# Attention scores of both row halves in one two-bank PSUM tile, with one mask addition for four heads, in a two-layer decoder trunk

## The chip, the core and the metric

The kernel runs on one core of a Trainium2 chip. The metric is the device time of one execution in microseconds (us), the median of several runs. The profile is that of one execution, taken by the hardware profiler: it gives each instruction's start and duration on each engine. The engines are TensorE (PE; its weight loads are listed as PEld), VectorE (DVE), ScalarE (ACT), GpSimd (POOL) and SyncE (SP), which only issues DMAs. PE writes its results to PSUM, which has eight banks; a bank holds 128 partitions x 512 fp32 values.

## The reference, cut to what matters

Two layers over 1024 tokens of width 1024, all in fp32. Layer 0 mixes with retention and RWKV-7 heads, layer 1 with sliding-window attention; a SwiGLU FFN follows each, and a final norm. The change touches the attention of layer 1:

```python
q = q.reshape(B, NB, W, SWA_KV_HEADS, SWA_GROUP, HEAD_DIM)      # 8 blocks of W = 128, 4 groups of 4 heads, 64 wide
...
kb, vb = with_prev(k), with_prev(v)                             # the block before and the block: 256 keys
s = jnp.einsum('bnqhgd,bnkhd->bnhgqk', q, kb).astype(jnp.float32) * HEAD_DIM ** -0.5
...
s = jnp.where(valid[None, :, None, None], s, -jnp.inf)          # the band of 128 keys
m = jnp.maximum(jnp.max(s, axis=-1, keepdims=True), sink)
e = jnp.exp(s - m)
p = e / (jnp.sum(e, axis=-1, keepdims=True) + jnp.exp(sink - m))
o = jnp.einsum('bnhgqk,bnkhd->bnqhgd', p.astype(vb.dtype), vb)
return o.reshape(B, T, SWA_WIDTH) @ w_o + b_o
```

## The kernel before, in words

The 1024 tokens are worked in two halves of 512 (half 0 and half 1), with features on the partitions. Large matmuls ("gemms": `gemm`, lines 341 to 347, and `prod`, lines 1166 to 1171) split each fp32 operand into a high and a low part and run three matmuls per 128 x 512 tile. The FFN of a layer has an "early" stage (`ffn_early`), which needs half 0 alone, and a "late" stage (`ffn_late`, `late`), which needs both halves; its down projection (`down`) comes after.

In `attn` (lines 1490 to 1592), called once for each half, K and V are projected first. `kc` holds the keys of two KV heads on partitions 0 to 63 and 64 to 127, and `ks` the same with the two swapped. Then come four groups of four heads (`g`) with two projections of Q each (`proj(i, ...)` for i = 2g, 2g+1; a tile `qt` holds one head on partitions 0 to 63 and one on 64 to 127), and in each group four blocks of 128 queries (`b`). For one group and block:

- The scores (lines 1539 to 1547). For each half of the partitions, `e` = 0 or 1, there is a PSUM tile of its own, tag `r` for e = 0 and `c` for e = 1, one buffer of one bank each. Two matmuls (i = 0, 1) contract 64 rows, those of partitions 64e to 64e + 63, so e = 0 uses the upper and e = 1 the lower rows of PE's array. The matmuls are in plain fp32; each shows as two instructions in the trace. A block has 256 keys; the first block of half 0 has 128.
- The mask (line 1548): after each `e`, one DVE addition adds `amask` to its two heads and writes them to the SBUF tile `s`.
- The softmax (lines 1554 to 1569): maximum over all four heads on DVE (`tensor_reduce`), four exponentials on ACT, then normalisation on DVE.
- Transposes on PE into PSUM tag `m` (line 1574), copied out by ACT (1576) and DVE (1578); probabilities times V on PE into tag `y` (line 1584); the split into high and low parts by ACT and DVE (1590, 1591).

`w_o` (line 1594) then multiplies the output projection in tag `f`.

The order of the work on each engine is fixed when the kernel is built: the tile framework orders instructions by their place in the program and by when, on an estimated timeline, their operands and buffers are ready (line 1821). So the gemms of other stages stand between those of the attention on PE. At run time each engine follows its list in order and waits where something is late. In `trunk`, `rest_d(1, ...)` (the end of layer 0's FFN for half 1) runs beside attention of half 0, and the early FFN of layer 1 (lines 1740 to 1742) beside attention of half 1.

PSUM tiles come from a pool with a fixed number of buffers for each tag. One pool, opened at line 1711 between the early and late FFN of layer 0 (`f` 3, `m` 2, `r` 1, `c` 1, `y` 1: eight banks), serves everything after, to line 1770. Pools are opened with `reuse_waits="tile"` (line 233): a tile in the place of a closed pool's tile waits for that tile's last use. The late FFN (lines 1287 and 1288) uses two tiles of tag `m`, one of `r` and one of `c`; the early FFN of layer 1 uses `f` and, from its seventh pair, `m`.

Of the kernel before, what the change touches and what calls it, by code (L numbers as in the profile page):

```python
# [13 lines left out]
ALU = mybir.AluOpType  # L14
AX = mybir.AxisListType

P = 128
# [187 lines left out]
class Kern:  # L205
# [1284 lines left out]
    def attn(self, hf, nr, ap, n8):  # L1490
        nc = self.nc
        nT, r = nr
        V, S, G = nc.vector, nc.scalar, nc.gpsimd
        ident = self.cst["ident"]
        amask, sink, b8 = self.amask, self.sink, self.b8

        def proj(ti, out, **kw):
            w = self.wload(self.A["w_qkv"][ti])
            ps = self.pst("f", [P, HT])
            self.gemm(ps, w, nT)  # L1500
            V.tensor_tensor(out=out, in0=ps, in1=r, op=ALU.mult)
            S.activation(out, out, AF.Identity, **kw)

        kc, ks = [], []
        for i in range(2):
            kt = self.t(ap, [P, P + HT], f"kc{i}", 2)
            proj(8 + i, kt[:, P:], bias=self.col("bqkv", 8 + i))
            st = self.t(ap, [P, P + HT], f"ks{i}", 1)
            lo = 0 if hf else P
            if hf:  # L1510
                G.tensor_copy(kt[:, 0:P], self.pk[i][:, HT : HT + P])
            nc.sync.dma_start(st[0:64, lo:], kt[64:128, lo:])
            nc.sync.dma_start(st[64:128, lo:], kt[0:64, lo:])
            kc.append(kt)
            ks.append(st)
        vt = self.t(ap, [P, 5, 256], "vt", 2)
        if hf:
            G.tensor_copy(vt[:, 0, :], self.pvt[:, 4, :])
        vcs = [self.t(ap, [P, HT], "s", 3) for _ in range(2)]
        for i, vc in enumerate(vcs):  # L1520
            proj(10 + i, vc, bias=self.col("bqkv", 10 + i))
        for i, vc in enumerate(vcs):
            pt = self.pst("m", [P, 4, P])
            for b in range(4):
                nc.tensor.transpose(pt[:, b, :], vc[:, P * b : P * b + P], ident)
            S.copy(vt[:, 1:5, P * i : P * i + P], pt)
        self.pk, self.pvt = kc, vt
        q8 = self.s8(ap, "q8", 2)
        qt = [q8[i // 4][:, i % 4, :] for i in range(8)]
        for g in range(4):  # L1530
            for i in (2 * g, 2 * g + 1):
                proj(i, qt[i], scale=0.125, bias=b8[:, i : i + 1])
            for b in range(4):
                ti, rg = g // 2, g % 2
                k0 = 1 if (hf == 0 and b == 0) else 0
                kw = slice(P * k0, 256)
                nk = 256 - P * k0
                s = self.t(ap, [P, 4, 256], "s", 3)
                for e in range(2):
                    ps = self.pst("rc"[e], [P, 2, 256])  # L1540
                    a = slice(64 * e, 64 * e + 64)
                    src = (kc if e == rg else ks)[ti]
                    for i in range(2):
                        nc.tensor.matmul(
                            ps[:, i, kw], qt[2 * g + i][a, P * b : P * b + P], src[a, P * b + P * k0 : P * b + 256],
                            start=True, stop=True,
                        )
                    V.tensor_tensor(
                        out=s.rearrange("p (i e) k -> p e i k", e=2)[:, e, :, kw], in0=ps[:, :, kw],
                        in1=amask[:, kw].rearrange("p (o t) -> p o t", o=1).to_broadcast([P, 2, nk]), op=ALU.add,  # L1550
                    )
                st4 = self.t(ap, [P, 32], "st4", 4)[:, :16].rearrange("p (a b) -> p a b", b=4)
                m, den, es = st4[:, 0, :], st4[:, 1, :], st4[:, 2, :]
                V.tensor_reduce(out=m, in_=s[:, :, kw], axis=AX.X, op=ALU.max)
                sk = sink[:, 4 * g : 4 * g + 4]
                V.tensor_tensor(out=m, in0=m, in1=sk, op=ALU.max)
                V.tensor_tensor(out=es, in0=sk, in1=m, op=ALU.subtract)
                V.tensor_scalar(out=m, in0=m, scalar1=-1.0, scalar2=None, op0=ALU.mult)
                S.activation(es, es, AF.Exp)
                for h in range(4):  # L1560
                    S.activation(
                        s[:, h, kw], s[:, h, kw], AF.Exp, bias=m[:, h : h + 1], accum_out=den[:, h : h + 1]
                    )
                V.tensor_tensor(out=den, in0=den, in1=es, op=ALU.add)
                V.reciprocal(out=den, in_=den)
                for h in range(4):
                    V.tensor_scalar(
                        out=s[:, h, kw], in0=s[:, h, kw], scalar1=den[:, h : h + 1], scalar2=None, op0=ALU.mult
                    )
                pT = self.t(ap, [P, 2, 4, P], "pT", 3)  # L1570
                for kb in range(k0, 2):
                    pt = self.pst("m", [P, 4, P])
                    for h in range(4):
                        nc.tensor.transpose(pt[:, h, :], s[:, h, P * kb : P * kb + P], ident)
                    if kb == 0:
                        S.copy(pT[:, kb], pt)
                    else:
                        V.tensor_copy(pT[:, kb], pt)
                po = self.pst("y", [P, 2, P])
                for e in range(2):  # L1580
                    a = slice(64 * e, 64 * e + 64)
                    pv4 = pT.rearrange("p k (i e) t -> p k e i t", e=2)
                    for kb in range(k0, 2):
                        nc.tensor.matmul(
                            po[a], vt[:, b + kb, 64 * g : 64 * g + 64], pv4[:, kb, e],
                            start=kb == k0, stop=kb == 1,
                        )
                tk = slice(P * b, P * b + P)
                hi, lo_ = n8[g][:, :, tk], n8[4 + g][:, :, tk]
                S.copy(hi, po)  # L1590
                V.tensor_tensor(out=lo_, in0=po, in1=hi.bitcast(F32), op=ALU.subtract)
        return [self.hl(n8, k) for k in range(KT)]
# [42 lines left out]
def trunk(tc, A, out):  # L1635
    with ExitStack() as ctx:
        K = Kern(ctx, tc, A, out)
# [4 lines left out]
        def close(*gs):  # L1642
            for g in gs:
                g.__exit__(None, None, None)
# [15 lines left out]
        def ffn_late(L, sp, stage, opened):  # L1660
            gs, wp, ws = opened
            K.w6 = True
            xs, ts, raws = K.stage(stage)
            wp.append(raws)
            q, X = deque(), []
            nf = DGROUPS[L][-1][1]

            def next_w():
                while len(q) < 5:
                    w = next(ws, None)  # L1670
                    if w is None:
                        break
                    q.append(w)
                return q.popleft()

            for p in range(NP):
                f = K.form_down(L, p - 1, xs[(p - 1) % 2], ts) if 0 < p <= nf else iter(range(5))
                if L and p == NP - 1:
                    f = both(f, K.first_x(L, wp, X))
                K.ffn_pair(L, p, sp, next_w, f, xs[p % 2])  # L1680
            close(*gs)
            K.w6 = False
            return xs[(NP - 1) % 2], ts, X
# [6 lines left out]
        def early(L, sp, lo, hi, form=None, steps=1):  # L1690
            for p in range(lo, hi):
                K.lo = tc.nc.vector if form else tc.nc.gpsimd
                K.ffn_early(L, p, sp, "ff" if L and p < 6 else "fm")
                K.lo = tc.nc.gpsimd
                for _ in range(steps if form else 0):
                    next(form, None)
# [7 lines left out]
        r = K.factor_of(1, sp, "c")  # L1704
# [6 lines left out]
        gp = K.psum("ps", {"f": 3, "m": 2, "r": 1, "c": 1, "y": 1})  # L1711
        ffn_late(0, sp, K.pp, opened)
        close(gc, gs, gb)
        gf, fp = K.pool("fa", "left")
        gz, fz = K.pool("fz", "left")
# [7 lines left out]
        run(K.rest_d(0, X[0], fp, raws))  # L1723
        K.wx = None
        ws = [K.wsplit(K.rest_w(1, d), len(X[1]) * P) for d in range(2)]
        close(gz, gf)
        g1, nB = K.pool("nB", "right")
        ga, ap = K.pool("at", "right")
        K.attn_open(ap)
# [2 lines left out]
        f = K.rest_d(1, X[1], stop=2, ws=ws)  # L1732
# [11 lines left out]
        r = K.factor_of(1, sp)  # L1744
# [5 lines left out]
        f = K.form1("n2b", r, K.n8(K.pp), cb, ft)  # L1750
# [3 lines left out]
        close(gt)  # L1754
        opened = late_open(1)
        early(1, sp, NP - 1, NP)
        x, ts, X = ffn_late(1, sp, nB, opened)
        close(gs, gc)
        gz, fz = K.pool("fz", "left")
# [66 lines left out]
```

## Time and profile before

| | before |
|---|---|
| median of 3 runs, us | 2411.41 (2411.33 to 2417.5) |
| the profiled execution's own time, us | 2407.97 |
| its span, first to last instruction, us | 2406.2 |
| DVE, ACT, POOL busy, us | 1631.0, 1036.0, 1208.5 |
| DMA, mean over the span | 165 GB/s |
| mean granted TensorE clock | 0.988 |

In the views that follow, a line of the timeline gives the start in us from the span's start, the time from first start to last end of the instructions merged in it, the engine, the line of the kernel, the operation, output <- inputs by the program's names with shapes, and the count. In the busy table by stretch, each engine has its busy us and the number of its instructions, and at the end come the clock that PE was granted (1.00 is full), the share of DMA time and GB/s. A group's row gives count, busy us, mean ns of one, and the idle time before. The durations of matmuls overlap, since they are pipelined.

### The profile page before, as it was taken

To read this page: it belongs to the slowest core of one execution; us is meant where nothing else is said; L and a number is where in the kernel's file an instruction comes from. 1 tells how busy PE (TensorE), PEld (TensorE's weight loads), DVE (VectorE), ACT (ScalarE), POOL (GpSimd) and SP (SyncE) were. 2 spreads that over 40 slices of the span, in tenths; PEclk is the share of its full clock that TensorE was granted. 3 is DMA by queue.
4 is the path that set the end of the run, shared out by engine and by line. 5 is a ranking of instruction groups with operands and counts; after the bars stand their busy time and mean duration, and the time that the engine had idled before them with its cause. 6 is when DMAs were issued, how large, how long until landed. Compare 5 with 4: busy or idle time off the path is not lost. (4 is left out here: it accounts for less than half of the span.)

```text
span 2406.2 us, 35718 instructions
## 1 busy us (share of the span) xinstructions
PE 2327.4 (97%) x13098; PEld 1836.9 (76%) x13098; DVE 1631.0 (68%) x2478; ACT 1036.0 (43%) x1914; POOL 1208.5 (50%) x975
## 2 busy tenths in 40 slices
PE   8899999989999999999999999999999999999997
PEld 6676767777777888888778877677688788887785
DVE  5766765766557457887675459558628788888666
ACT  5353543223555433333333545456635233333336
POOL 6555332221443047776577632342231677777666
PEclk9999999999999999999999999999999999999999
DMA  7564543444345645553564322132236466646652
GB/s 250 197 214 171 165 155 123 143 119 124 122 171 166 213 155 207 215 204 135 198 249 148 127 75 64 53 134 67 94 123 216 158 215 217 215 182 248 242 201 108
DMA packets 167742, 395.93 MB, mean 165 GB/s; under 512 B 42896, under 2 KB 45584, under 8 KB 167568
## 3 DMA queue, kind: packets, MB, share of 16 engines
q1 hardware_dynamic: 164448, 388.15, 47.5%
q10 hardware_dynamic: 2832, 4.45, 0.5%
q8 instruction: 104, 1.70, 0.3%
q0 software_dynamic: 288, 1.05, 0.1%
q14 instruction: 70, 0.57, 0.1%
HBM read 271.29 MB, written 116.92 MB: 161 GB/s over the span
## 5 line engine op out<-in xcount | busy, mean ns | idle before, releaser
L331 POOL TENSOR_TENSOR w<-wr,w 128x512 fp32r<-128x512 f32 x196 | 266.3, 1365 | 444.3 <-ACT w L330 386.7
L239 PE MATMUL ps_f<-n,w 128*128 128x512 f32 x1440 | 384.4, 415 | 13.6 <-ACT w L330 5.9
L239 PEld LDWEIGHTS ps_f<-n,w 128*128 128x128 f32 x1440 | 268.4, 192 | 97.1 <-issue 22.0
L330 ACT CAST w<-wr 128x512 fp32r<-128x512 f32 x244 | 147.9, 612 | 180.1 <-PE ps_f L347 74.1
L331 POOL TENSOR_TENSOR w<-wq,w 128x512 fp32r<-128x512 f32 x92 | 130.0, 1424 | 32.6 <-ACT w L330 28.1
L345 PE MATMUL ps_f<-n,w 128*128 128x512 f32 x356 | 141.6, 398 | 2.4 <-ACT n L351 1.5
L346 PE MATMUL ps_f<-n,w 128*128 128x512 f32 x356 | 142.0, 399 | 0.0
L347 PE MATMUL ps_f<-n,w 128*128 128x512 f32 x356 | 140.5, 395 | 0.0
L1169 PE MATMUL ps_f<-n,w 128*128 128x512 f32 x322 | 127.1, 396 | 4.5 <-DVE h L1369 2.2
L1176 DVE TENSOR_TENSOR nq<-ps_m,u 128x512 f32<-128x512 f32 x88 | 58.8, 684 | 105.8 <-PE ps_m L1171 105.7
L1170 PE MATMUL ps_f<-n,w 128*128 128x512 f32 x322 | 126.3, 392 | 0.0
L1171 PE MATMUL ps_f<-n,w 128*128 128x512 f32 x322 | 125.6, 391 | 0.0
L353 POOL TENSOR_TENSOR n<-nq,n 128x512 fp32r<-128x512 f32 x64 | 107.0, 1684 | 10.7 <-ACT n L351 10.7
L1169 PE MATMUL ps_m<-n,w 128*128 128x512 f32 x282 | 110.5, 392 | 0.0
L1171 PE MATMUL ps_m<-n,w 128*128 128x512 f32 x282 | 109.9, 390 | 0.0
L1170 PE MATMUL ps_m<-n,w 128*128 128x512 f32 x282 | 109.7, 389 | 0.0
L331 POOL TENSOR_TENSOR wx<-wr,wx 128x512 fp32r<-128x512 f32 (+1 forms) x38 | 49.3, 1298 | 104.4 <-ACT wx L330 97.7
L1169 PE MATMUL ps_m<-cb,w 128*128 128x512 f32 x240 | 93.5, 389 | 0.9 <-DVE nq L1176 0.9
L1170 PE MATMUL ps_m<-cb,w 128*128 128x512 f32 x240 | 93.4, 389 | 0.0
L1171 PE MATMUL ps_m<-cb,w 128*128 128x512 f32 x240 | 93.4, 389 | 0.0
L1343 POOL TENSOR_TENSOR w<-wd,w 128x512 fp32r<-128x512 f32 (+1 forms) x53 | 76.5, 1455 | 33.3 <-ACT w L1342 33.3
L345 PEld LDWEIGHTS ps_f<-n,w 128*128 128x128 f32 x356 | 67.1, 189 | 20.1 <-issue 2.2
(525 smaller groups left out, 6496.8 us busy)
## 6 DMA issues: line engine op xcount, KB each, us to landing
hc<-n SPq DMA_DIRECT2D x74, 512.0 KB, 2.6
wsp<-w SPq DMA_DIRECT2D x54, 512.0 KB, 3.4
w<-wsp SPq DMA_DIRECT2D x54, 512.0 KB, 3.8
wq<-in_w_gate SPq DMA_DIRECT2D x44, 512.0 KB, 4.3
u<-u SPq DMA_DIRECT2D x88, 256.0 KB, 3.0
n<-hc SPq DMA_DIRECT2D x43, 512.0 KB, 5.4
wr<-in_w_in SPq DMA_DIRECT2D x34, 512.0 KB, 4.6
hid<-n SPq DMA_DIRECT2D x66, 256.0 KB, 2.0
```

The source lines that it names most:

```text
L239: self.nc.tensor.matmul(out, lhsT, rhs, **kw)
L330: nc.scalar.copy(hi[:, :n], raw[:, c])
L331: self.lo.tensor_tensor(out=lo[:, :n], in0=raw[:, c], in1=hi.bitcast(F32)[:, :n], op=ALU.subtract)
L345: nc.tensor.matmul(ps, hi, rh, start=k == 0, stop=False)
L346: nc.tensor.matmul(ps, hi, rl, start=False, stop=False)
L347: nc.tensor.matmul(ps, lo, rh, start=False, stop=k == n - 1)
L353: e.tensor_tensor(out=lo, in0=src, in1=hi.bitcast(F32), op=ALU.subtract)
L1169: mm(ps, hi, xh, start=first and k == 0, stop=False, skip_group_check=True)
L1170: mm(ps, hi, xl, start=False, stop=False, skip_group_check=True)
L1171: mm(ps, lo, xh, start=False, stop=last and k == len(w) - 1, skip_group_check=True)
L1176: add = lambda o, x, y: V.tensor_tensor(out=o, in0=x, in1=y, op=ALU.add)
L1343: nc.gpsimd.tensor_tensor(out=lo, in0=v, in1=hi.bitcast(F32), op=ALU.subtract)
```

## The change

The scores of both row halves go into one PSUM tile of two banks, tag `rc`, one buffer: the first bank for e = 0, the second for e = 1. The matmuls are issued with `i` outermost, so the two halves take turns. One DVE addition then adds the mask to all four heads. Since tag `rc` takes the place of `r` and `c` in the attention, the PSUM pool is closed before the attention and one with `rc` is opened, and closed again after the last early FFN pair of layer 1, where one with `r` and `c` is opened for the late FFN.

```diff
-                for e in range(2):
-                    ps = self.pst("rc"[e], [P, 2, 256])
-                    a = slice(64 * e, 64 * e + 64)
-                    src = (kc if e == rg else ks)[ti]
-                    for i in range(2):
+                ps = self.pst("rc", [P, 2, 2, 256])
+                for i in range(2):
+                    for e in range(2):
+                        a = slice(64 * e, 64 * e + 64)
+                        src = (kc if e == rg else ks)[ti]
                         nc.tensor.matmul(
-                            ps[:, i, kw], qt[2 * g + i][a, P * b : P * b + P], src[a, P * b + P * k0 : P * b + 256],
+                            ps[:, e, i, kw], qt[2 * g + i][a, P * b : P * b + P], src[a, P * b + P * k0 : P * b + 256],
                             start=True, stop=True,
                         )
-                    V.tensor_tensor(
-                        out=s.rearrange("p (i e) k -> p e i k", e=2)[:, e, :, kw], in0=ps[:, :, kw],
-                        in1=amask[:, kw].rearrange("p (o t) -> p o t", o=1).to_broadcast([P, 2, nk]), op=ALU.add,
-                    )
+                V.tensor_tensor(
+                    out=s.rearrange("p (i e) k -> p e i k", e=2)[:, :, :, kw], in0=ps[:, :, :, kw],
+                    in1=amask[:, kw].rearrange("p (o u t) -> p o u t", o=1, u=1).to_broadcast([P, 2, 2, nk]),
+                    op=ALU.add,
+                )
@@ trunk, before the attention
-        close(gz, gf)
+        close(gz, gf, gp)
+        gp = K.psum("pa", {"f": 3, "m": 2, "rc": 1, "y": 1})
@@ trunk, before ffn_late of layer 1
         early(1, sp, NP - 1, NP)
+        close(gp)
+        gp = K.psum("pc", {"f": 3, "m": 2, "r": 1, "c": 1, "y": 1})
         x, ts, X = ffn_late(1, sp, nB, opened)
```

## The prediction

> **What bounds the kernel now.** I read the page first, then busy time by stretch around the attention, then the timeline of the score matmuls there, then what PE waits for.
>
> ```profile
> span 2406.2 us, 35718 instructions
> PE 2327.4 (97%) x13098; PEld 1836.9 (76%) x13098; DVE 1631.0 (68%) x2478; ACT 1036.0 (43%) x1914; POOL 1208.5 (50%) x975
> ```
>
> ```profile
> core 0: us, PE busy (x) PEld busy (x) DVE busy (x) ACT busy (x) POOL busy (x), PEclk, DMA share, GB/s
> 1400.00:1514.00 114.00, 114.00 (x589) 82.50 (x587) 95.53 (x221) 65.00 (x201) 33.10 (x28) 1.00 0.19 59
> 1514.00:1535.00 21.00, 15.46 (x88) 9.72 (x88) 9.96 (x29) 7.85 (x21) 1.27 (x1) 0.93 0.08 26
> 1595.00:1760.00 165.00, 162.98 (x831) 118.01 (x831) 105.63 (x237) 92.67 (x246) 48.12 (x37) 1.00 0.25 85
> 855.00:885.00 30.00, 30.00 (x134) 24.85 (x133) 15.76 (x18) 9.54 (x17) 16.36 (x13) 1.00 0.59 194
> 1855.00:1885.00 30.00, 27.85 (x115) 22.20 (x114) 23.10 (x25) 8.72 (x16) 19.18 (x13) 0.94 0.56 193
> ```
>
> PE is busy for 97% of the span. The attention of row half 0 lies at 1400 to 1535 us, that of half 1 at 1595 to 1760. Until 1514 PE has no gap: whenever the attention chain isn't ready, the scheduled order gives PE matmuls of the projections, of the layer-0 rest and, in half 1, of the next FFN. From 1514 to 1535 this filler has run out and PE idles 5.54 us. DVE is the next engine: 95.53 of 114 us, or 84%, in half 0, but 64% (105.63 of 165) in half 1. So PE time is what to count, and in half 0's end also DVE's.
>
> **Part 1: what the new order does to PE.** The eight score instructions of a 128-query block (four fp32 matmuls, two passes each) look different from block to block:
>
> ```profile
> L1544 PE MATMUL ps_r<-kc,q x64: 272/376/480, 1403.2 to 1685.5; 64*128 64x256 f32 x56, 64*128 64x128 f32 x8
> ```
>
> ```profile
> 1507.61 1.13 PE L1544 MATMUL ps_r<-ks,q 64*128 64x256 f32 x4
> 1508.66 0.50 PE L347 MATMUL ps_f<-n,wx 128*128 128x512 f32 x1
> 1509.10 1.13 PE L1544 MATMUL ps_c<-kc,q 64*128 64x256 f32 x4
> 1510.15 0.49 PE L345 MATMUL ps_f<-n,wx 128*128 128x512 f32 x1
> ```
>
> ```profile
> 1652.81 0.48 PE L1544 MATMUL ps_r<-ks,q 64*128 64x256 f32 x1
> 1652.82 0.48 PE L1544 MATMUL ps_c<-kc,q 64*128 64x256 f32 x1
> ...
> 1653.57 0.38 PE L1544 MATMUL ps_c<-kc,q 64*128 64x256 f32 x1
> 1653.88 0.50 PE L347 MATMUL ps_f<-n,wx 128*128 128x512 f32 x1
> ```
>
> The row is one of four alike (two sources, two banks): 256 instructions, 8 for each of 32 blocks, 4 blocks of them with 128 keys (the first block of half 0, four head groups). At 1507 the halves run apart: 1.13 us for one, a gemm matmul, 1.13 us for the other. At 1652 they alternate and start 0.01 us apart: the two row halves of the array work at once, and the whole block takes 1653.57 + 0.38 - 1652.81 = 1.14 us. A block pays twice because its halves have a bank and a mask addition each: the first bank comes free an addition earlier, and the scheduler sends that half alone. In the new form all four matmuls wait for the one two-bank tile, so they become ready together. What all blocks cost now stands in one row for each attention half, and the cost of a paired short block follows it:
>
> ```profile
> 1400.00:1535.00 135.00, 21.83 (x128) 13.49 (x128) 0.99 0.18 53
> 1595.00:1735.00 140.00, 24.86 (x128) 14.40 (x128) 1.00 0.24 79
> ```
>
> ```profile
> 1487.04 0.37 PE L1544 MATMUL ps_r<-ks,q 64*128 64x128 f32 x1
> ...
> 1487.49 0.27 PE L1544 MATMUL ps_c<-kc,q 64*128 64x128 f32 x1
> ```
>
> These windows count line 1544 alone. A paired short block takes 1487.49 + 0.27 - 1487.04 = 0.72 us. With every block paired, half 0 takes 12 x 1.14 + 4 x 0.72 = 16.6 us instead of 21.83, a gain of 5.3; half 1 takes 16 x 1.14 = 18.2 instead of 24.86, a gain of 6.6; together 11.9. Not every block will stay whole: the matmuls with i=0 need only the first of two query projections, and a ready matmul of an earlier block can come between, as here:
>
> ```profile
> 1645.13 0.70 PE L1544 MATMUL ps_r<-ks,q 64*128 64x256 f32 x2
> 1645.76 1.10 PE L1574 MATMUL ps_m<-c_ident,s 128*128 128x128 f32 x8
> ```
>
> Two matmul passes of one half alone take 0.70 us, and a pair of halves costs the same, so a block split by i costs 2 x 0.70 - 1.14 = 0.26 us more. I allow six split blocks, an estimate: 1.6 us. That leaves 4.5 us for half 0 and 5.8 for half 1.
>
> How much reaches the end? In half 1 all of it: the last attention matmuls end at about 1755, and the filler (line 1169, FFN) is not used up then:
>
> ```profile
> 1754.29 1.09 PE L1584 MATMUL ps_y<-pT,vt 128*64 128x256 f32 x8
> ...
> 1799.01 0.39 PE L1169 MATMUL ps_f<-n,w 128*128 128x512 f32 x1
> ```
>
> So 5.8 us. In half 0 the filler ends at 1514 and the end is set by the chain through DVE, so PE's gain there is capped by what DVE gains, which is part 2.
>
> **Part 2: the mask addition.** Two additions of two heads become one of four, over both banks.
>
> ```profile
> L1554 DVE TENSOR_REDUCE st<-s 128x4 f32<-128x1024 f32 x12 | 14.5, 1211 | 0.1
> L1548 DVE TENSOR_TENSOR s<-ps_r,c_amask 128x512 f32<-128x512 f32 x12 | 8.2, 681 | 1.7 <-PE ps_c L1544 1.7
> L1548 DVE TENSOR_TENSOR s<-ps_r,c_amask 128x256 f32<-128x256 f32 x4 | 1.7, 413 | 0.0
> ```
>
> From 256 to 512 elements the addition grows by 0.268 us, so 1024 take 0.681 + 2 x 0.268 = 1.22 us, an estimate from these rows that the 1.211 us of the 1024-element reduction supports. Reading across two banks in one instruction isn't in the trace; its bounds are that 1.21 and two of today's, 1.36. I take 1.22, the nearest row: 0.14 us less per block, 2.3 us in 16 blocks. In half 1 DVE is 64% busy and this is hidden. In half 0 I count these 2.3 us, and 4.5 is the upper bound.
>
> The new wait: the next block's scores stand until the whole addition is over, 1.22 us after its start; before, the first half could start after 0.68 and the second after 1.36. Queued behind the waiting scores on PE are the gemms placed after them; the scheduler puts filler ahead of them instead, as it does now. While there is filler this costs nothing; without it, a block can lose up to 1.22 us (a rival below).
>
> **Part 3: the PSUM pools opened anew.** Before the attention a new pool holds 3+2+2+1 banks, and after it another holds 3+2+1+1+1; eight both times, and no tag loses a buffer except the shared score tile. Reuse waits are per tile. Before the attention the banks that the new tiles take were last used by finished FFN work or by gemms that are evacuated as they go: nothing, with one drain (below) as the bound. The second opening stands between the early and late FFN of layer 1. There PE waits now:
>
> ```profile
> PE ps_m L1169 <- DVE sg L1220: 2.1, 1, 2.1
> ```
>
> The late FFN's `m` bank is still held by the last early product until DVE has multiplied it out, and PE has nothing else; the clock falls to 0.94 over 30 us, 1.8 us more. In layer 0 the same two stages have a pool opened between them already, and there PE is busy 30.00 of 30.00 us at clock 1.00 (855 to 885). With the new pool, `m` begins in other banks than the ones the early products hold if banks are handed out by first use. Bounds: no gain, or 2.1 + 1.8 = 3.9. Nearest is layer 0's row, no wait; I take the 2.1 and leave the clock to the range.
>
> **The sum.** 5.8 + 2.3 + 2.1 = 10.2 us. The profiled execution's 2407.97 us (the span of 2406.2 and 1.8 around it) becomes 2397.8; it lies 3.4 below the median of 2411.41, from which I subtract the same: 2401.2.
>
> **Rivals.** This measurement can tell about 0.3%, 7.2 us, from no change: faster is under 2404.2, slower over 2418.6.
>
> *Slower: no cover for the new wait.* If the blocks follow each other in lockstep in half 0, each of 16 loses 1.22 us: 19.5 - 11.9 = 7.6 us slower, about 2419. It decides from the 10th exposed block on (11.9 / 1.22). For it: 5.54 us of idle PE after 1514, where the filler is gone already, and a PE that finishes filler sooner reaches that point sooner. Against: 114.00 of 114.00 us before, and filler left after half 1.
>
> *The pairing doesn't come.* The scheduler splits nearly all blocks by i: 32 x 0.26 = 8.3 of the 11.9 are lost, and 3.6 remain: about 2408. For it: 1645. Against: the waits that split the halves now are gone.
>
> *A drain at each opening.* If a new pool waits for the last matmul of the old one, each opening costs a wait like that at 1870, 2.1 us with 1.8 of clock. The second keeps the one that it has now, so the 2.1 is not won; the first adds 3.9, and 8.1 - 3.9 = 4.2 remain: 2407. Against it is layer 0's opening.
>
> *Strict order on PE.* In this visit the second half came late:
>
> ```profile
> 1700.17 0.48 PE L1544 MATMUL ps_r<-ks,q 64*128 64x256 f32 x1
> 1700.43 0.48 PE L1544 MATMUL ps_c<-kc,q 64*128 64x256 f32 x1
> 1700.49 0.59 PE L1544 MATMUL ps_r<-ks,q 64*128 64x256 f32 x2
> 1700.75 0.38 PE L1544 MATMUL ps_c<-kc,q 64*128 64x256 f32 x1
> ```
>
> Each half keeps its own pace, 0.32 us from first to second pass (1700.17 to 1700.49, 1700.43 to 1700.75), as if it had a queue of its own; then the order of issue doesn't matter. If instead matmuls start strictly in order, and the new order issues both passes of a matmul together, a first pass shares its step only with the pass before it: eight passes take five steps instead of four, one step of (1653.57 - 1652.82 - 0.32) / 2 = 0.21 us more for each of 32 blocks, 6.7 us lost at most, and 10.2 - 6.7 = 3.5 remain: about 2408. The Trainium skill ("TensorE: Matmul & The Clock Gate", under "The mechanism" of row and column tiling) has the rule that matmuls start and end strictly in program order, whatever their row group. The trace can't exclude it, for a stream issued alternately would look alike at 1652, but 1700 speaks against it.
>
> **How the numbers follow.** The forecast has 0.62, slower 0.08; pairing lost 0.10, drain 0.12, strict order 0.08, all three within 0.3%. Faster 0.62, same 0.30, slower 0.08. The lower end takes 11.9 + 3.9 and 1.5 of clock (0.07 x 21) in half 0, 2394, and one half-clock stretch of 1.8 gone elsewhere: 2392. The upper end is no gain at all and one new wait of 2.1, since every engine's order is made anew: 2414. That leaves out the slower case and little more.
>
> **What would show it.** Right: score visits with both halves in nearly every block; line 1544 busy about 36 us instead of 46.7; 32 mask additions of about 1.2 us; PE still full in half 1; no wait of the first late `m` bank; PE idling a little more at the end of half 0. Wrong: as many lone halves as now, new PE waits on the mask addition, or idle PE at the openings.

## The result and the profile after

The changed kernel takes 2398.97 us, the median of 6 runs (2392.07 to 2401.51), beside 2412.66 us of the kernel before (6 runs, 2411.33 to 2419.89). The ratio is 0.9941, 95% interval 0.9925 to 0.9957: 10 to 18 us faster. The forecast was 2401.2, faster. One execution among those below took 8005.62 us and is left out of the medians and ratios.

The busy time by stretch, after (columns as before: length; busy us and count of PE, PEld, DVE, ACT, POOL; clock, DMA share, GB/s):

```profile
1400.00:1514.00 114.00, 114.00 (x602) 81.27 (x601) 86.05 (x196) 63.02 (x187) 36.32 (x30) 1.00 0.19 60
1510.00:1535.00 25.00, 21.02 (x116) 13.28 (x116) 17.56 (x49) 12.40 (x39) 3.57 (x3) 1.00 0.07 22
1595.00:1760.00 165.00, 165.00 (x873) 122.16 (x872) 100.50 (x227) 92.86 (x248) 53.74 (x42) 1.00 0.26 90
1840.00:1870.00 30.00, 27.57 (x116) 22.32 (x114) 23.16 (x22) 8.51 (x15) 18.73 (x13) 0.94 0.64 227
```

In the first and third row PE starts more instructions in the same time than before (602 instead of 589, 873 instead of 831). It idles 3.98 us at the end of half 0 instead of 5.54, and in half 1 not at all. The last row is the begin of the late FFN: there PE still loses 2.4 us, and the clock is at 0.94 as before.

The score matmuls alone, in the same two stretches as in the prediction:

```profile
1400.00:1535.00 135.00, 17.70 (x128) 10.63 (x128) 1.00 0.17 53
1595.00:1735.00 140.00, 18.42 (x128) 10.93 (x128) 1.00 0.25 85
```

That is 36.1 us instead of 46.7. A block of the timeline of PE, after:

```profile
1676.53 0.48 PE L1544 MATMUL ps_rc<-kc,q 64*128 64x256 f32 x1
1676.54 0.48 PE L1544 MATMUL ps_rc<-ks,q 64*128 64x256 f32 x1
...
1677.29 0.38 PE L1544 MATMUL ps_rc<-ks,q 64*128 64x256 f32 x1
1677.59 0.50 PE L1170 MATMUL ps_f<-n,w 128*128 128x512 f32 x1
```

`kc` and `ks` are the two row halves; they start 0.01 us apart and the block takes 1677.29 + 0.38 - 1676.53 = 1.14 us. In the kernel before, the two halves stood wholly apart in seven of the 32 blocks and partly in six; now in none wholly. Four blocks are still split: three by `i`, and in one, at 1459 us, the first matmul of one half goes alone. The mask addition (28 full blocks; the four short ones take 0.682 us each), and what PE waits for from 1380 to 1740 us (total us, times, longest), after:

```profile
L1548 DVE TENSOR_TENSOR s<-ps_rc,c_amask 128x1024 f32<-128x1024 f32 x28 | 34.0, 1215 | 6.5 <-PE ps_rc L1544 6.4
```

```profile
PE ps_y L1585 <- DVE n L1592: 1.9, 1, 1.9
PE ps_m L1575 <- DVE s L1568: 1.0, 1, 1.0
PE ps_y L1585 <- ACT pT L1577: 0.6, 1, 0.6
PE ps_f L345 <- ACT n L1591: 0.5, 1, 0.5
```

The waits add up to 4.0 us, all in half 0. In the kernel before they were 7.2, in five kinds:

```profile
PE ps_y L1584 <- DVE n L1591: 1.9, 2, 0.9
PE ps_m L1574 <- DVE pT L1578: 1.7, 2, 0.9
PE ps_m L1574 <- ACT pT L1576: 1.7, 3, 0.6
PE ps_y L1584 <- DVE st L1556: 1.0, 1, 1.0
PE ps_f L345 <- ACT n L1590: 0.9, 2, 0.5
```

**Where the time went.** PE runs the same number of instructions in both kernels, so the same count of them marks the same amount of work: between two counts lie as many matmuls of each shape in the one as in the other. Number 8,500, just before the attention, and number 10,850, after it, counted from 0, are these, two rows of before and two of after:

```profile
1372.41 0.39 PE L347 MATMUL ps_f<-n,w 128*128 128x512 f32 x1
...
1864.73 0.39 PE L1170 MATMUL ps_m<-n,w 128*128 128x512 f32 x1
```

```profile
1375.95 0.39 PE L347 MATMUL ps_f<-n,w 128*128 128x512 f32 x1
...
1853.24 0.39 PE L1170 MATMUL ps_m<-n,w 128*128 128x512 f32 x1
```

Between them lie 492.3 us before and 477.3 after, a gain of 15.0. The parts: score matmuls 46.7 - 36.1 = 10.6; PE waits 7.2 - 4.0 = 3.2; and the clock at the end of half 0, 0.93 over 21 us before and 1.00 after, 1.5. Together 15.3. By halves the parts close less well: between numbers 8,500 and 9,300 (half 0) the changed kernel gains 163.4 - 158.1 = 5.3 us, and between 9,500 and 10,400 (half 1) 180.5 - 170.8 = 9.7, where the parts make about 7 and 8.4. So the good agreement of the sums is partly luck. The spans differ by 10.7 only, because in this execution the changed kernel came to the attention 3.5 us later (1375.95 against 1372.41), where PE's list of instructions is still the same in both. In the profiled executions below this first mark lies anywhere from 1370.8 to 1379.1, so a kernel's time carries several us that have nothing to do with the attention.

### The profile page after: what moved, and what is told of

Same layout as the page of the kernel before. It is cut to its first block, busy times and chain, and to the rows that moved or that the text cites. A ratio compares the mean times of both kernels' runs of the same rounds, so it can differ in the third digit from the quotient of the medians.

```text
span 2395.5 us, 35700 instructions
## 1 busy us (share of the span) xinstructions
PE 2317.0 (97%) x13098; PEld 1829.0 (76%) x13098; DVE 1619.7 (68%) x2446; ACT 1034.8 (43%) x1912; POOL 1208.2 (50%) x975
## 4 chain that ended last, share of the span: by engine, by line
PE 73%; DVE 10%; DMA 5%; ACT 4%; issue 4%; POOL 3%; SPq 1%; DVEq 0%; ACTq 0%; POOLq 0%
PE ps_m L1169 7%; PE ps_m L1171 7%; PE ps_m L1170 7%; PE ps_f L239 6%; PE ps_f L346 5%; PE ps_f L345 5%; PE ps_f L347 5%; PE ps_m L239 4%; PE ps_f L1170 3%; PE ps_f L1169 3%; PE ps_f L1171 3%; PE ps_r L1169 2%; PE ps_c L1169 2%; PE ps_r L1170 2%; PE ps_c L1171 2%
## 5 line engine op out<-in xcount | busy, mean ns | idle before, releaser
L1176 DVE TENSOR_TENSOR nq<-ps_m,u 128x512 f32<-128x512 f32 x88 | 58.6, 684 | 104.9 <-PE ps_m L1171 104.7
```

What stands on the lines that cost most here:

```text
L1176: add = lambda o, x, y: V.tensor_tensor(out=o, in0=x, in1=y, op=ALU.add)
```

## The experiments

The theory after the result: the gain is the pairing of the row halves, brought by the common tile. Rivals: the single addition, the order of issue, the new pools. All ratios are to runs of the kernel before on the same chip; the changed kernel's is 0.9941, and differences from it are taken between these ratios, at 2411 us. By the intervals such a difference is good to about 5 us. The time between counted instructions of PE is much finer, and stands at the end of this section.

**The pools alone.** The attention as before, and

```diff
-        close(gz, gf)
+        close(gz, gf, gp)
+        gp = K.psum("pa", {"f": 3, "m": 2, "r": 1, "c": 1, "y": 1})
...
+        close(gp)
+        gp = K.psum("pc", {"f": 3, "m": 2, "r": 1, "c": 1, "y": 1})
         x, ts, X = ffn_late(1, sp, nB, opened)
```

> The kernel before, with both PSUM pools opened anew at the two places of the change (banks f 3, m 2, r 1, c 1, y 1 both times), and the attention as before. Theory of pairing (the gain comes from score matmuls of both row halves standing together on PE): within 2 us of before; line 1544 stays busy about 46.7 us with lone halves; the PE wait of a late m bank on DVE line 1220 (2.1 us) goes, but a wait of the third late product on DVE line 1176 of about 2.4 us takes its place, as in the changed kernel. Theory of the pools (freeing the m banks is worth a good part of it): 3 to 4 us faster than before, no PE wait over 1 us between 1850 and 1880 us.

Measured: 2409.52 us, ratio 0.9989 (0.9977 to 1.0001). By the interval the pools are worth up to 5.5 us, and by count nothing; no drain shows at the first opening (number 8,500 starts at 1370.8 us, earlier than in the kernel before). PE's wait at the begin of the late FFN, in this run:

```profile
PE ps_m L1169 <- DVE nq L1176: 2.4, 1, 2.4
```

The wait for the held bank (DVE L1220, 2.1 us) is gone, and one of 2.4 us for another DVE instruction has taken its place, as the theory of pairing had it.

**One tile, two additions.** The changed kernel, with the addition in two parts:

```diff
-                V.tensor_tensor(
-                    out=s.rearrange("p (i e) k -> p e i k", e=2)[:, :, :, kw], in0=ps[:, :, :, kw],
...
+                for e in range(2):
+                    V.tensor_tensor(
+                        out=s.rearrange("p (i e) k -> p e i k", e=2)[:, e, :, kw], in0=ps[:, e, :, kw],
...
```

> The changed kernel, with the mask added in two instructions of two heads each, out of the one two-bank tile. Theory of pairing: both banks still come free together, so nearly every block stays paired, line 1544 is busy 37 to 38 us, and the time is 0 to 3 us above the changed kernel's (2.3 us of DVE time in half 0): 10.5 to 14 us faster than before. Theory of the addition (one DVE instruction for two is what pays): half or more of the gain is lost, 7 us or less faster than before.

Measured: 2397.02 us, ratio 0.9940 (0.9924 to 0.9957). The scores take 35.9 us (17.44 + 18.42): the pairing comes with the common tile and doesn't need the single addition. By the medians no time is lost either, but the profiled execution was the slowest of the six (2404.99 us), and PE waits there for 9.9 us instead of 4.0, most of it for DVE:

```profile
PE ps_y L1585 <- DVE n L1592: 4.4, 5, 1.8
PE ps_m L1575 <- DVE s L1568: 3.5, 7, 1.1
PE ps_f L345 <- ACT n L1591: 1.0, 2, 0.5
```

By count half 0 keeps its whole gain (158.0 us), but half 1 takes 177.9 us instead of 170.8. So 7 of the 15 us between the marks hang on the single addition or on the order that was made with it. The second addition is only about 0.14 us of DVE time in a block, 2.3 us in 16, so the order probably has a part; how much is not shown.

**The order of issue, two tiles.** The kernel before, with `i` outermost and both additions behind:

```diff
+                pse = [self.pst("rc"[e], [P, 2, 256]) for e in range(2)]
+                for i in range(2):
+                    for e in range(2):
...
+                            pse[e][:, i, kw], ...
+                for e in range(2):
+                    V.tensor_tensor(...)
```

> The kernel before with i as the outer loop of the score matmuls and both mask additions after them, still two tiles of one bank each and the old pool. Theory of pairing: the first bank still comes free an addition before the second, so lone halves remain, line 1544 is busy over 43 us, and the time is within 4 us of before. Theory of the order of issue (taking turns is what makes the halves run together): line 1544 busy near 37 us, 8 us or more faster than before.

Measured: 2405.95 us, ratio 0.9969 (0.9956 to 0.9981), 4.6 to 10.6 us faster than before. The scores take 46.4 us (21.38 + 25.00), with lone halves as before: the pairing theory was right on the scores and wrong on the time, which it put within 4 us. Something other than pairing pays here.

**The additions behind, e outermost.** The same with the two loops exchanged back, to tell apart the two edits in that run.

> The kernel before with both mask additions placed after the matmuls of both row halves, e still the outer loop, two tiles and the old pool: the run with i outermost minus its order. If that run's 5 us came from the place of the additions in the program: the same here, 2404 to 2407. If they came from i being outermost: within 2 us of before. In both, line 1544 stays busy over 45 us.

Measured: 2411.53 us, ratio 1.0003 (0.9987 to 1.0019), scores 46.7 us. So it was `i` outermost. What it changes shows in half 1, first this run, then the one with `i` outermost:

```profile
1595.00:1760.00 165.00, 162.97 (x833) 117.85 (x832) 108.54 (x241) 94.15 (x248) 50.97 (x39) 1.00 0.24 86
```

```profile
1595.00:1760.00 165.00, 165.00 (x845) 120.14 (x844) 103.57 (x241) 91.99 (x247) 50.91 (x40) 1.00 0.25 88
```

The 2.0 us in which PE waited are gone, as in the changed kernel (165.00). The schedule is made anew with any edit, and this order happens to leave no wait there. By count half 1 is 2.9 us shorter than before (177.6 instead of 180.5). Half 0 takes 162.8 us; it took 163.4 in the kernel before, and 166.0 and 165.8 in the two runs that differ from it in the pools or the place of the additions alone. Those two were granted a clock of 0.96 over 1400 to 1540 us, the kernel before and this run 0.99, the changed kernel 1.00. So the count finds 3.4 of the 7.5 us beside the kernel before and 5.9 beside the additions behind, part of it in the clock.

**One tile, e outermost.** The changed kernel with only the loops exchanged:

```diff
-                for i in range(2):
-                    for e in range(2):
+                for e in range(2):
+                    for i in range(2):
```

> The changed kernel with e as the outer loop: both matmuls of the first row half are issued before both of the second, into the one two-bank tile. If each row half of PE keeps its own pace whatever the order of issue: starts alternate 0.01 us apart as in the changed kernel, a full block takes 1.14 us, and the time is within 2 us of the changed kernel. If matmuls start strictly in the order of issue: the four passes of one half end before the other half starts, a block takes about 2.0 us, line 1544 is busy over 60 us, and the time is 10 us or more above the changed kernel's, near or above that of before.

Measured: 2399.92 us, ratio 0.9943 (0.9930 to 0.9956), as the changed kernel by the ratios; by count half 1 is 4.1 us longer (174.9 instead of 170.8) and half 0 0.6. In PE's list of instructions, as the kernel is built, the last block has two matmuls on `ks` (i = 0, 1) and then two on `kc`, with nothing between. The same block in the timeline of this run:

```profile
1702.89 0.48 PE L1544 MATMUL ps_rc<-ks,q 64*128 64x256 f32 x1
1702.90 0.48 PE L1544 MATMUL ps_rc<-kc,q 64*128 64x256 f32 x1
1703.21 0.38 PE L1544 MATMUL ps_rc<-ks,q 64*128 64x256 f32 x1
1703.22 0.38 PE L1544 MATMUL ps_rc<-kc,q 64*128 64x256 f32 x1
...
1703.65 0.38 PE L1544 MATMUL ps_rc<-kc,q 64*128 64x256 f32 x1
```

All four passes on `ks` stand ahead of the first on `kc` in the list, and yet `kc` starts 0.01 us after the first of them. Each row half keeps its own order and doesn't wait for the other. The kernel before shows the same: its loop has `e` outermost too, and the block at 1652 us, whose halves alternate in the timeline, is listed as two matmuls of one half and then two of the other.

**What PE time is worth, half by half.** The changed kernel with every score matmul issued twice in one half of the attention, with the same output:

```diff
-                for i in range(2):
+                for i in (0, 1) * (2 if hf == 0 else 1):      # the other run: hf == 1
```

> The changed kernel with every score matmul of half 0 issued twice into the same place (the result is the same): per full block eight more passes, four steps of 0.215 us = 0.86 us, half that in the four short blocks, 12.1 us of PE in all. Theory that PE sets the pace in half 0 too: 9 to 13 us slower than the changed kernel (its 4.0 us of idle PE there can hide a little). Theory of the prediction (the chain through DVE sets the end of half 0, so PE time counts for about half): 6 us slower or less.

> The same in half 1: 16 x 0.86 = 13.8 us more of PE. Both theories (PE is full in half 1): 12 to 15 us slower than the changed kernel. If a wait or DVE were the bound there: 6 us or less.

Measured: half 0 2408.08 us, ratio 0.9990 (0.9976 to 1.0005), 11.8 us above the changed kernel; half 1 2413.96 us, ratio 1.0010 (1.0000 to 1.0020), 16.6 above it. Line 1544 is busy 32.88 instead of 17.70 us in the one and 34.83 instead of 18.42 in the other. So 15.2 us of PE cost 11.8 in half 0, and 16.4 cost 16.6 in half 1, each give or take 5. By count they cost 173.3 - 158.1 = 15.2 in half 0 and 190.2 - 170.8 = 19.4 in half 1, a short stretch of lower clock included in each.

**What DVE time is worth: a miss, and again.** The first form was four additions of the mask to itself in each block:

```diff
+                if hf == 0:                                    # the other run: hf == 1
+                    dd = self.t(ap, [P, 256], "dd", 1)
+                    for _ in range(4):
+                        V.tensor_tensor(out=dd, in0=amask, in1=amask, op=ALU.add)
```

> The changed kernel with four additions of 256 elements into an unused tile in each block of half 0, DVE work that nothing reads: at 0.25 to 0.33 us each, 16 to 21 us more of DVE, queued in front of the maximum. Theory that PE sets the pace: 5 us slower or less, taken up by DVE's idle time. Theory of the prediction (DVE's chain sets the end of half 0): 10 us or more slower.

> The same in half 1, where DVE is busy for 61% of the time: both theories 0 to 3 us slower than the changed kernel.

Measured: 2405.15 us, ratio 0.9978 (0.9963 to 0.9993), and 2404.86 us, ratio 0.9977 (0.9962 to 0.9992): the same for both. The additions depend on nothing in their block, and the scheduler put all 64 between 1362 and 1416 us, before half 0's softmax, in both runs. They tell nothing of either half. The second form hangs on the block's own reciprocals:

```diff
                 V.reciprocal(out=den, in_=den)
+                if hf == 0:                                    # the other run: hf == 1
+                    dd = self.t(ap, [P, 256], "dd", 1)
+                    for h in range(4):
+                        V.tensor_scalar(out=dd, in0=amask, scalar1=den[:, h : h + 1], scalar2=None, op0=ALU.mult)
```

> The changed kernel with four more DVE multiplications of 256 elements in each block of half 0, by the block's own reciprocals, so that they can't be moved out of the attention; nothing reads their result. Like the normalisation of 256 elements beside them they take 0.28 to 0.38 us each: 18 to 24 us more of DVE in 16 blocks, in front of the normalisation. Theory that PE sets the pace in half 0 (the doubled scores cost about 9 us there for 12 us of PE): 6 us slower than the changed kernel or less, taken up by DVE's idle time. Theory of the prediction (the chain through DVE sets the end of half 0): 10 us or more slower.

> The same in half 1, where DVE is busy for 61% of 165 us and PE has filler to the end: both theories 0 to 3 us slower than the changed kernel.

Measured: half 0 2406.76 us, ratio 0.9975 (0.9963 to 0.9988), 8.2 us above the changed kernel, for this row:

```profile
L1570 DVE TENSOR_SCALAR dd<-c_amask,st 128x256 f32<-128x256 f32 x64 | 23.1, 360 | 0.4
```

In half 1, with 22.2 us of the same: 2398.92 us, ratio 0.9951 (0.9935 to 0.9966), 2.4 us above it, which can't be told from none. With an uncertainty of 5 us, 8.2 decides between neither theory (6 or less, 10 or more). By count half 0 is 166.1 - 158.1 = 8.0 us longer, and half 1 in the other run 3.7, so in half 0 neither theory holds alone. PE's waits of this run between 1380 and 1740 us show who is late:

```profile
PE ps_m L1579 <- DVE s L1572: 3.6, 4, 1.3
PE ps_y L1589 <- DVE n L1596: 3.5, 2, 3.2
PE ps_y L1589 <- DVE st L1566: 1.3, 1, 1.3
PE ps_rc L1544 <- DVE s L1548: 1.1, 3, 0.5
PE ps_y L1589 <- ACT pT L1581: 0.6, 1, 0.6
PE ps_f L345 <- ACT n L1595: 0.5, 1, 0.5
```

They are 10.6 us instead of 4.0, nearly all for DVE, and the scores wait for the mask addition (L1548), which they don't in the changed kernel.

**The wait that took the bank's place.** In the changed kernel DVE does this at the begin of the late FFN:

```profile
1856.84 0.67 DVE L1220 TENSOR_TENSOR sg<-sg,ps_m 128x512 f32<-128x512 f32 x1
1857.44 1.18 DVE L1202 TENSOR_TENSOR ws<-n 128x512 f32<-128x512 f32 x1
1858.66 1.67 DVE L1203 TENSOR_TENSOR n<-n,n 128x512 f32<-128x512 f32 x1
...
1862.05 1.64 DVE L1205 TENSOR_TENSOR n<-n 128x512 f32<-128x512 f32 x1
1863.61 1.28 DVE L1176 TENSOR_TENSOR nq<-ps_m,u 128x512 f32<-128x512 f32 x2
```

The four weight sums (L1202 to L1205) stand ahead of the addition that reads the first late product out of PSUM (L1176), and the third product goes into that bank. The edit lets ScalarE empty the bank, in the first pair alone:

```diff
         self.prod(b, w(), X["t2"], True, False)
-        add(u1, b, u0)
+        if act:                                  # L == 1 and p == 0
+            self.nc.scalar.copy(u1, b)
+            add(u1, u1, u0)
+        else:
+            add(u1, b, u0)
```

> The changed kernel with one edit in the late FFN of layer 1: in its first pair, ScalarE copies the first product out of PSUM, and the addition on DVE works on the copy, so the next product no longer waits for DVE. If the wait of 2.4 us at 1862 us is what the freed m banks turned into: it goes, and with it up to 1.8 us of clock: 2 to 4 us faster than the changed kernel, near 2396. Rival (the next thing is late as well, the halves of the weights or DVE's next addition): a wait of 1 us or more stands elsewhere between 1855 and 1875 us, and the time is within 1.5 us of the changed kernel.

Measured: 2392.58 us, ratio 0.9922 (0.9905 to 0.9940), 4.6 us below the changed kernel by the ratios, whose intervals overlap. PE's waits and busy time there:

```profile
PE ps_m L1169 <- DVE nq L1176: 0.8, 1, 0.8
```

```profile
1840.00:1870.00 30.00, 29.17 (x129) 23.81 (x129) 27.03 (x24) 10.62 (x19) 19.69 (x13) 1.00 0.65 228
```

PE starts 129 instructions in the 30 us instead of 116, and the clock stays at 1.00. This version has the lowest median of all that were run. From number 10,850 to the end it takes 538.1 us, the changed kernel 542.2. Part of that can be chance: the run with `e` outermost in one tile, which still has a wait of 2.3 us there, keeps the clock at 1.00 after it and takes 539.5.

**The same work by count, half by half.** Time in us between the starts of PE's instructions of these numbers, in the profiled execution of each run. A run with doubled scores has 128 more instructions in its half, which are counted in.

| run | half 0: 8,500 to 9,300 | half 1: 9,500 to 10,400 |
|---|---|---|
| before | 163.4 | 180.5 |
| pools alone | 166.0 | 180.4 |
| two tiles, additions behind, `e` outermost | 165.8 | 180.5 |
| two tiles, additions behind, `i` outermost | 162.8 | 177.6 |
| changed | 158.1 | 170.8 |
| one tile, two additions | 158.0 | 177.9 |
| one tile, `e` outermost | 158.7 | 174.9 |
| scores doubled in half 0 | 173.3 | 170.8 |
| scores doubled in half 1 | 158.0 | 190.2 |
| more DVE work in half 0 | 166.1 | 170.8 |
| more DVE work in half 1 | 158.1 | 174.5 |
| ScalarE empties the bank | 158.1 | 170.7 |

Where the attention of a half is the same, the times agree to 0.1 us, but for half 0 of the first three, where the clock differs. So these differences can be read to a fraction of a us, though each edit also makes the order of the work anew, and the differences hold that too.

## Why the prediction was right, and where not

- **The cost of lone halves, and the pairing** held: 36.1 us of score matmuls (forecast: about 36), no half wholly alone, four blocks split by `i` (forecast: six). That the common tile brings it is shown from both sides: one tile with two additions has no block with its halves wholly apart, two tiles with `i` outermost keep seven.
- **Half 1** held and was more. 24.86 - 18.42 = 6.4 us of PE time (forecast: 5.8), and the doubled scores show that it counts in full there. By count the half gains 9.7 us. Not foreseen were the 2.0 us of waits that went as well; the run with `i` outermost in two tiles, where they went without any change in pairing, shows that they can go by the new schedule alone. The other side of this is the run with two additions: paired as well (18.42 us), it keeps only 2.6 of the 9.7. So "DVE is 64% busy and this is hidden" holds for the changed kernel's order and not for every order.
- **Half 0 was the step that was undersized.** The prediction let the chain through DVE cap the gain at 2.3 us. The prices are 11.8 / 15.2, or 0.8, for a us of PE (1.0 by count, with that stretch of lower clock), and 8.2 / 23.1, or 0.35, for one of DVE: most of PE's time counts there, and a part of DVE's. By them PE's 21.83 - 17.70 = 4.1 us are worth 3.2 to 4.1 and DVE's 2.3 us 0.8, together 4.0 to 4.9, an estimate. Besides, the stretch of lower clock at the end of half 0 went, 1.5 us, which was left to the range. By count the half gains 5.3 us beside the kernel before, whose clock there was the better of the three executions.
- **The addition** held: 1.215 us (forecast: 1.22) in the 28 full blocks (the forecast named all 32), so reading across two banks costs nothing extra here. What the single addition gains in time isn't settled: nothing by the medians, up to 7 us in half 1 by count, the order included.
- **The pools: the step that failed.** "With the new pool, `m` begins in other banks" held, and the 2.1 us didn't come: the prediction asked which bank was late and not what DVE has to do next. The instruction that frees the bank for the third product was queued behind the same kind of weight sums. With that wait removed as well the median is 4.6 us lower, though the intervals overlap.
- **The rivals.** No drain (pools alone); pairing came; the new wait costs nothing in the changed kernel, since no wait of the scores on the addition is in its list, but the DVE load in half 0 shows that the cover there is short. Strict order on PE is refuted by the run with `e` outermost, and already by the block at 1652 us, which the prediction took for undecided though the loop of the kernel before issues one half first: the Trainium skill ("TensorE: Matmul & The Clock Gate", under "The mechanism") has matmuls start in program order whatever their row group, and here a matmul of the other row group started 0.01 us after the first of four passes that stood ahead of it. The measurement decides.
- **The sum.** 10.2 forecast, 10 to 18 measured. What was too low: half 0 with its clock, the waits of half 1; what was too high: the pools. That the 2.1 us of the pools, which didn't come, are nearly the 2.0 us of waits in half 1, which nobody forecast, is luck.

Open: of the 7.5 us that `i` outermost brings in two tiles, 3.4 to 5.9 are found by count. In one tile the same order adds nothing by the ratios (0.9941 with it, 0.9943 without) and 4.8 us by count. Each edit makes the order of the work anew, which moves half 1 by several us, and no run parts the order from the edit; so of the 15 us between the marks the 10.6 us of paired scores are shown, and the rest belongs to this order of the work.

## What to carry to other kernels

In this kernel two matmuls that use different row halves of PE ran at once where they stood together in PE's list, even when one came 0.26 us late (at 1700 us). They stood apart where the scheduler put other work between them. So give them buffers that come free together, and look in the timeline for the halves that stand alone. Whether PE time counts in a stage is told by doubling it there, and extra work for such a test must hang on data of that stage, or the scheduler moves it out. When runs of one kernel differ by more than the effect, compare the times between the same counted instructions. When a buffer is freed, look at the queue of the engine that frees the next one.

## What the runs showed of the hardware

The row halves of PE each follow their own order, as shown above: four passes of one half issued first don't hold back the other.

The same DVE operation on two SBUF operands takes 0.69 us or 1.67 us. The first two rows are DVE's in the kernel before, the next three are POOL's of the same time:

```profile
1861.86 0.69 DVE L1204 TENSOR_TENSOR wq<-ws,wq 128x512 f32<-128x512 f32 x1
1865.62 1.67 DVE L1204 TENSOR_TENSOR wq<-ws,wq 128x512 f32<-128x512 f32 x1
```

```profile
1859.54 1.74 POOL L331 TENSOR_TENSOR w<-ws,w 128x512 fp32r<-128x512 f32 x1
1863.29 1.75 POOL L331 TENSOR_TENSOR wr<-wq,wr 128x512 fp32r<-128x512 f32 x1 [2.01 <-ACT wr L330]
1865.00 1.74 POOL L331 TENSOR_TENSOR wr<-ws,wr 128x512 fp32r<-128x512 f32 x1
```

At 1861.86 POOL stands idle between its first two, at 1865.62 it is at work. The Trainium skill ("SBUF — State Buffer", under "Who interferes with whom") has a DVE instruction with two SBUF inputs contend with a GpSimd instruction that reads SBUF, and these times agree with it. In the changed kernel three of the four weight sums ahead of the late bank's addition take 1.64 to 1.67 us; that the 2.4 us of wait come about in this way was read from the rows and not tried.
